# Token mixing of a two-layer hybrid backbone: whole-head score banks, bursts of small products, and work moved between engines

## The chip, the core and the metric

One core of one Trainium2 chip runs the whole program in one launch. The time is device microseconds (us) of that core, the median over runs. The engines are named as in the profile: PE is the matrix engine and PEld its weight loads, DVE the vector engine, ACT the scalar engine, POOL is GpSimd, SP issues most transfers.

## What is computed

Two layers of a hybrid backbone run over 1024 latent tokens and 256 context tokens of width 1024. Each layer mixes tokens and then applies a gated convolutional feed-forward network. The change is in the mixing, whose parts are these (from the reference, cut):

```python
def attend(q, k, v):
    s = jnp.einsum('bhgqd,bhkd->bhgqk', q, k).astype(jnp.float32) * (HEAD_DIM ** -0.5)
    p = jax.nn.softmax(s, axis=-1).astype(v.dtype)
    return jnp.einsum('bhgqk,bhkd->bhgqd', p, v)
...
def gla_scan(q, k, v, logf, s0, reverse):
    ...
    def step(state, inp):
        ...
        scores = jnp.einsum('bhtk,bhtsk,bhsk->bhts', qc, decay, kc)
        o = (jnp.einsum('bhts,bhsv->bhtv', scores, vc)
             + jnp.einsum('bhtk,bhkv->bhtv', qc * jnp.exp(cum), state))
```

There are eight attention heads of width 64. A latent token reads 1280 keys, a context token 256. The recurrence has four heads and runs forward and backward, with a decay for every channel. A Fourier mix over the tokens is the third part. The three results are joined and pass through one output projection.

## The kernel before

**Stages.** In each layer the kernel projects the queries, keys and forget gates (`project_qkv`), and then starts the attention as a generator that is laced with whatever else the mixing has to do: the remaining projections (`project_rest`), the Fourier mix (`fourier`), the recurrence (`recurrence`) and the first output tiles. `interleave` advances the attention in proportion to shares in the table `LACE`. The feed-forward network follows. In the profiled execution the attention of the first layer lies between about 286 and 757 us and its recurrence between 520 and 750 us; in the second layer the attention lies between 2037 and 2467 us and the recurrence between 2280 and 2465 us.

**What sets the order.** Each engine takes its instructions strictly in a fixed order. A scheduler makes that order ahead of time from the order of the code, the dependencies, and a priority: `ahead("qk")` and the like move the instructions of a `with` block forward by the number in the table `AHEAD`. An instruction that stands early and is not ready holds up everything behind it on its engine.

**Attention.** `score(i, pr)` handles two heads of one 128-row tile. For one head it takes the 1280 keys in pieces of 512, 512 and 256. Each piece has a PSUM bank of its own (tag `s`, three banks, used in turn), two products on PE into it (L567 and L568), and a maximum over the piece on DVE (L570). A fourth small maximum joins the three (L573). Then ACT takes the exponential of each piece (L577), which also reads out a sum. `value(i, pr)` transposes the exponentials on PE (`ps_t`, L603), splits them into a rounded part `ph` (ACT, L608) and a rest `pl` (DVE, L609), and multiplies both with the values (`ps_o`, L613 and L615).

**Recurrence.** `pair_steps(i)` handles two tiles of 128 tokens, and at most two pairs are in work at once. A pair goes through seven levels. A level forms small products of the decayed queries and keys (`scores`, tile `psc`, L774): 64 channels deep, 32 or 64 tokens wide, 16 or 32 of them for a level, alternately for the two halves `e` of the channels, each half in a PSUM bank of its own (tag `g`, two banks, which the other small results of the mixing use too). In the profile each of these products is two matrix instructions. The results go into `near` (L857), `next` (L861) or `at` (L864). Then four products with the decays update the tile `W` for the next level (L876): the one with `w == 0` on DVE, the other three on POOL. At the level of 32 tokens eight copies on DVE put `near` and `next` into `at` (L868). `kc` is copied from `W` on ACT (L838) for the next level's products.

## Time and profile before

| what | value |
|---|---|
| median of 3 runs | 3351.05 us (3343.71 to 3359.85) |
| the profiled execution, its own time | 3347.55 us |
| its span in the trace | 3345.0 us |
| PE busy, share of the span | 3087.2 us, 92% |
| DVE busy | 2379.1 us, 71% |
| ACT busy | 1581.3 us, 47% |
| POOL busy | 780.8 us, 23% |
| granted clock of PE, mean | 0.973 |

The shares are means over stages that differ. PE counts as busy as long as any matrix instruction is in flight, from the start of the first to the modelled end of the last. A time between two starts on PE therefore tells more of what an instruction costs than its own length does, since the instructions overlap.

### The profile page before, as it was taken

What the parts mean: (1) busy time and instruction counts of PE and PEld (TensorE: products, weight loads), DVE (VectorE), ACT (ScalarE), POOL (GpSimd) and SP (SyncE); (2) the same over time, 40 slices, a digit from 0 to 9 for tenths busy, and PEclk for the clock granted to TensorE, in tenths of its full rate; (3) what the DMA queues carried; (4) which work ended last, traced back from release to release, by engine and by line L of the source; (5) the groups of instructions that cost most, each with busy time, mean ns of one, the idle gap of its engine ahead of it and who ended that gap; (6) DMA issues with size and microseconds to landing.
All of it is one profiled execution on the core that took longest, in us unless ns stands there. A gap on an engine that the chain in (4) does not pass through costs nothing.

```text
span 3345.0 us, 55178 instructions
## 1 busy us (share of the span) xinstructions
PE 3087.2 (92%) x20897; PEld 2517.1 (75%) x20897; DVE 2379.1 (71%) x4377; ACT 1581.3 (47%) x3169; POOL 780.8 (23%) x820
## 2 busy tenths in 40 slices
PE   6999998999979999899999999998988789999996
PEld 4878977787756777677798788876766577887785
DVE  4624567887688877567876754668877778887678
ACT  3324556674444444334464435655652435554332
POOL 3522114432210000021245351115435200000222
PEclk9999998999989999999999999999999899999998
DMA  7652232107665444597775432122035632223973
GB/s 216 193 164 81 61 98 58 39 16 227 210 196 164 128 131 128 167 244 196 232 215 177 133 101 76 46 86 76 20 98 168 208 111 85 86 76 116 276 187 126
DMA packets 449215, 452.83 MB, mean 135 GB/s; under 512 B 31731, under 2 KB 343476, under 8 KB 448950
## 3 DMA queue, kind: packets, MB, share of 16 engines
q1 hardware_dynamic: 420118, 405.05, 38.6%
q0 software_dynamic: 28832, 44.27, 7.1%
q8 instruction: 164, 2.69, 0.3%
q14 instruction: 101, 0.83, 0.1%
HBM read 354.68 MB, written 94.54 MB: 134 GB/s over the span
## 4 chain that ended last, share of the span: by engine, by line
PE 46%; DVE 12%; DMA 5%; POOL 3%; issue 2%; ACT 2%; SPq 0%; POOLq 0%; DVEq 0%; ACTq 0%
PE pu L159 8%; PE pu L160 8%; PE pu L161 8%; PE pd L159 3%; PE pd L160 3%; PE pd L161 3%; PE ps_t L603 2%; DMA araw<-act 2%; DVE cv L1106 1%; PE ps_s L567 1%; PE ps_o L613 1%; PE ps_s L568 1%; PE ps_o L615 1%; PE pws L159 1%; DVE wlo L1373 1%
## 5 line engine op out<-in xcount | busy, mean ns | idle before, releaser
L570 DVE TENSOR_REDUCE mx<-ps_s 128x1 f32<-128x512 f32 (+1 forms) x400 | 222.0, 587 | 104.6 <-PE ps_s L568 103.3
L1331 POOL DMA_DIRECT2D X<-in_w_down_dram x48 | 57.0, 1188 | 1022.5 <-DMA X<-in_w_down_dram 944.7
L609 DVE TENSOR_TENSOR pl<-ps_t,ph 128x512 fp32r<-128x512 f32 x328 | 222.8, 685 | 84.1 <-ACT ph L608 82.2
L603 PE MATMUL ps_t<-ident,p 128*128 128x128 f32 x1312 | 260.2, 282 | 13.7 <-DVE pl L609 8.1
L577 ACT ACTIVATE p<-ps_s,mx 128x512 f32<-128x512 f32 (+1 forms) x400 | 242.4, 615 | 52.7 <-DVE mx L573 43.2
L608 ACT CAST ph<-ps_t 128x512 fp32r<-128x512 f32 x328 | 190.5, 588 | 158.8 <-PE ps_o L615 81.8
L160 PE MATMUL pd<-wlo,whi 128*128 128x512 f32 x616 | 248.6, 404 | 14.6 <-DVE wlo L1373 12.9
L159 PE MATMUL pd<-whi,wlo 128*128 128x512 f32 x616 | 243.6, 402 | 17.5 <-DVE wlo L1373 10.4
L1106 DVE SCALAR_TENSOR_TENSOR cv<-U,cw,cv 128x512 f32<-128x512 f32 x352 | 246.7, 746 | 12.8 <-ACT cv L1103 12.7
L161 PE MATMUL pd<-whi 128*128 128x512 f32 x616 | 248.1, 403 | 0.0
L159 PE MATMUL pxs<-whi,hlo 128*128 128x256 f32 x752 | 220.9, 294 | 5.7 <-DVE hraw L1552 4.3
L145 POOL TENSOR_TENSOR wlo<-raw,whi 128x1024 fp32r<-128x1024 f32 x63 | 153.5, 2439 | 281.1 <-ACT whi L144 281.0
L160 PE MATMUL pxs<-wlo,hhi 128*128 128x256 f32 x752 | 215.9, 287 | 0.5 <-DVE wlo L145 0.4
L161 PE MATMUL pxs<-whi,hhi 128*128 128x256 f32 x752 | 215.8, 287 | 0.0
L613 PE MATMUL ps_o<-pl,V 128*128 128x256 f32 x656 | 199.5, 321 | 7.0 <-DVE pl L609 4.1
L603 PEld LDWEIGHTS ps_t<-ident,p 128*128 128x128 f32 x1312 | 163.8, 142 | 36.8 <-DVE pl L609 11.1
L1103 ACT ACTIVATE cv<-U,cb,cw 128x512 f32<-128x512 f32 x176 | 137.6, 812 | 111.8 <-DVE U L1234 99.4
L615 PE MATMUL ps_o<-ph,V 128*128 128x256 f32 x656 | 182.0, 295 | 0.0
L1218 ACT CAST whi<-S 128x512 fp32r<-128x512 f32 x176 | 106.1, 618 | 146.4 <-PE pu L161 110.4
L144 ACT CAST whi<-raw 128x1024 fp32r<-128x1024 f32 x130 | 135.8, 1047 | 81.9 <-DMA raw<-in_w_up_dram 30.1
L567 PE MATMUL ps_s<-KT,qt 128*128 128x512 f32 (+1 forms) x400 | 149.8, 405 | 6.5 <-ACT p L577 3.1
L159 PEld LDWEIGHTS pd<-whi,wlo 128*128 128x128 f32 x616 | 117.6, 192 | 49.7 <-DVE wlo L1373 13.1
(398 smaller groups left out, 9191.7 us busy)
## 6 DMA issues: line engine op xcount, KB each, us to landing
raw<-in_w_up_dram SPq DMA_DIRECT2D x144, 512.0 KB
raw<-in_w_ada_dram SPq DMA_DIRECT2D x96, 512.0 KB
raw<-in_w_down_dram SPq DMA_DIRECT2D x52, 512.0 KB
act<-cv SPq DMA_DIRECT2D x88, 256.0 KB
X<-in_w_down_dram POOLq DMA_DIRECT2D x40, 512.0 KB, 9.7
raw<-in_w_in_dram SPq DMA_DIRECT2D x36, 512.0 KB
y<-r SPq DMA_DIRECT2D x28, 512.0 KB
araw<-act SPq DMA_DIRECT2D x26, 512.0 KB
```

What stands on the lines that cost most here:

```text
L159: nc.tensor.matmul(o, lhsT=al, rhs=bh, start=start, stop=False, skip_group_check=onto)
L160: nc.tensor.matmul(o, lhsT=ah, rhs=bl, start=False, stop=False, skip_group_check=onto)
L161: nc.tensor.matmul(o, lhsT=ah, rhs=bh, start=False, stop=stop, skip_group_check=onto)
L567: nc.tensor.matmul(t[:, 0:n], lhsT=qt[:, h % (2 * QT_PAIRS), :], rhs=KT[:, 2 * kv + 1, s0:s0 + n], start=True, stop=False)
L570: nc.vector.tensor_reduce(out=mx[:, j:j + 1], in_=t[:, 0:n], axis=AX.X, op=ALU.max)
L577: nc.scalar.activation(out=t, in_=sc[j][:, 0:n], func=AF.Exp, bias=mx[:, 3:4], accum_out=su[:, h, j:j + 1])
L603: nc.tensor.transpose(t[:, ss, h, :], in_=ps2[h][2 * s2 + ss], identity=ident)
L608: nc.scalar.copy(ph, tv)
L609: nc.vector.tensor_tensor(out=pl, in0=tv, in1=f32(ph), op=ALU.subtract)
L613: nc.tensor.matmul(o, lhsT=V[:, s, kv, 1:3, :].rearrange("p a c -> p (a c)"), rhs=pl[:, ss, :], start=(s == 0), stop=False)
L615: nc.tensor.matmul(o, lhsT=V[:, s, kv, 0:2, :].rearrange("p a c -> p (a c)"), rhs=ph[:, ss, :], start=False, stop=(s == nk - 1))
L1106: nc.vector.scalar_tensor_tensor(out=o, in0=u[:, tap:tap + n], scalar=convw[l][tap][:, c:c + 1], in1=o, op0=ALU.mult, op1=ALU.add)
```

## The change

- `score`: one tile of three banks holds all scores of a head; there is one such tile (`bufs=1`). The products stand as before, two for each bank. One maximum over all 1280 scores and one exponential over them follow, with one sum. The exponentials of a head lie in one buffer, five of these in all (before ten of 512 and five of 256, the same bytes).
- `AHEAD`: the score products, the maximum, the exponential and the small products of the recurrence all get 200 in both layers.
- `scores`: the half `e = 1` now comes first, and all other products of a call are ordered behind that first one (`tc.issue_after`).
- `pair_steps`: all four products with the decays go to POOL where outputs are needed (the one with `w == 2` stays on DVE for context tiles of the last layer), and the eight copies into `at` go to ACT.

```diff
--- before.py
+++ after.py
@@ -49,8 +49,8 @@
     {"p1": 0.578, "ft": 0.08, "hg": 0.38, "p3": 6.415, "pair": 3.177, "lead": 8.4},
 )
 AHEAD = (
-    {"qk": 50, "max": 100, "exp": 0, "pt": 50, "split": 0, "pv": 0, "kc": 0, "psc": 0, "ev": 50, "w": 0},
-    {"qk": 150, "max": 50, "exp": 0, "pt": 30, "split": 0, "pv": 0, "kc": 10, "psc": 0, "ev": 0, "w": 30},
+    {"qk": 200, "max": 200, "exp": 200, "pt": 50, "split": 0, "pv": 0, "kc": 0, "psc": 200, "ev": 50, "w": 0},
+    {"qk": 200, "max": 200, "exp": 200, "pt": 30, "split": 0, "pv": 0, "kc": 10, "psc": 200, "ev": 0, "w": 30},
 )
 R_AT = (4, 6)
 DOWN_AT = ((("P34", "P35", "P23", "P24"), ("P21", "P22", "P24", "P25"), ("P21", "P22", "P24", "P25"), ("P21", "P22", "P23", "P24")),
@@ -60,7 +60,7 @@
 QT_PAIRS = 1
 QT_BUFS = 3
 IN_WP = 2
-P_BUFS = {512: 10, 256: 5}
+P_BUFS = 5
 
 C_Q, C_KV, C_HQ, C_HI, C_FF, C_FB, C_HG, C_FT = 0, 512, 768, 1024, 1280, 1536, 1792, 2048
 
@@ -545,10 +545,9 @@
 
         def score(i, pr):
             nk = keys(i)
-            segs = [(s, min(512, nk * P - s)) for s in range(0, nk * P, 512)]
-            ns = len(segs)
+            n = nk * P
             if pr == 0:
-                su = ap.tile([P, NH, 3], F32, tag="su", bufs=2, name="su")
+                su = ap.tile([P, NH], F32, tag="su", bufs=2, name="su")
                 state["su", i] = su
             su = state["su", i]
             if pr % QT_PAIRS == 0:
@@ -559,31 +558,26 @@
             kv = pr // 2
             ps2 = []
             for h in (2 * pr, 2 * pr + 1):
-                mx = ap.tile([P, 4], F32, tag="mx", bufs=4, name="mx")
-                sc, p = [], []
-                for j, (s0, n) in enumerate(segs):
-                    t = psn.tile([P, 512], F32, tag="s", bufs=3, name="ps_s")
+
+                mx = ap.tile([P, 1], F32, tag="mx", bufs=4, name="mx")
+                t = psn.tile([P, 3 * 512], F32, tag="s", bufs=1, name="ps_s")
+                for s0 in range(0, n, 512):
+                    sl = slice(s0, min(n, s0 + 512))
                     with ahead("qk" if (i, pr) != units[0] else "pt"):
-                        nc.tensor.matmul(t[:, 0:n], lhsT=qt[:, h % (2 * QT_PAIRS), :], rhs=KT[:, 2 * kv + 1, s0:s0 + n], start=True, stop=False)
-                        nc.tensor.matmul(t[:, 0:n], lhsT=qt[:, h % (2 * QT_PAIRS), :], rhs=KT[:, 2 * kv, s0:s0 + n], start=False, stop=True)
-                    with ahead("max"):
-                        nc.vector.tensor_reduce(out=mx[:, j:j + 1], in_=t[:, 0:n], axis=AX.X, op=ALU.max)
-                    sc.append(t)
+                        nc.tensor.matmul(t[:, sl], lhsT=qt[:, h % (2 * QT_PAIRS), :], rhs=KT[:, 2 * kv + 1, sl], start=True, stop=False)
+                        nc.tensor.matmul(t[:, sl], lhsT=qt[:, h % (2 * QT_PAIRS), :], rhs=KT[:, 2 * kv, sl], start=False, stop=True)
                 with ahead("max"):
-                    nc.vector.tensor_reduce(out=mx[:, 3:4], in_=mx[:, 0:ns], axis=AX.X, op=ALU.max, negate=True)
-                for j, (s0, n) in enumerate(segs):
-                    t = ap.tile([P, n], F32, tag=f"p{n}", bufs=P_BUFS[n], name="p")
-                    with ahead("exp"):
-                        nc.scalar.activation(out=t, in_=sc[j][:, 0:n], func=AF.Exp, bias=mx[:, 3:4],
-                                             accum_out=su[:, h, j:j + 1])
-                    p += [t[:, c:c + P] for c in range(0, n, P)]
+                    nc.vector.tensor_reduce(out=mx, in_=t[:, 0:n], axis=AX.X, op=ALU.max, negate=True)
+                e = ap.tile([P, NT * P], F32, tag="p", bufs=P_BUFS, name="p")
+                with ahead("exp"):
+                    nc.scalar.activation(out=e[:, 0:n], in_=t[:, 0:n], func=AF.Exp, bias=mx, accum_out=su[:, h:h + 1])
+                p = [e[:, c:c + P] for c in range(0, n, P)]
                 ps2.append(p)
                 yield 0.84e-3 * nk * P
             state["p", i, pr] = ps2
             if pr == NH // 2 - 1:
                 rs = ap.tile([P, NH], F32, tag="rs", bufs=2, name="rs")
-                nc.vector.tensor_reduce(out=rs, in_=su[:, :, 0:ns], axis=AX.X, op=ALU.add)
-                nc.vector.reciprocal(out=rs, in_=rs)
+                nc.vector.reciprocal(out=rs, in_=su)
                 t = psn.tile([P, 512], F32, tag="g", bufs=2, name="ps_rs")
                 nc.tensor.transpose(t[0:NH, 0:P], in_=rs, identity=ident)
                 rt = ap.tile([NH, P], F32, tag="rst", bufs=2, name="rst")
@@ -767,12 +761,15 @@
 
 
             ts = [pg([P, 2, 2, size], "psc") for _ in range(2)]
-            for x in range(2):
-                for c in range(2):
-                    for b in range(0, P, size):
-                        for e in range(2):
-                            nc.tensor.matmul(ts[e][b:b + size, x, c, :], lhsT=keys(slice(64 * e, 64 * e + 64), c, x * P + b),
-                                             rhs=moving(slice(64 * e, 64 * e + 64), c, x * P + b), start=True, stop=True)
+            after = nullcontext()
+            for x, c, b, e in product(range(2), range(2), range(0, P, size), (1, 0)):
+
+                with after:
+                    m = nc.tensor.matmul(ts[e][b:b + size, x, c, :], lhsT=keys(slice(64 * e, 64 * e + 64), c, x * P + b),
+                                         rhs=moving(slice(64 * e, 64 * e + 64), c, x * P + b), start=True, stop=True)
+                if x == c == b == 0 and e:
+                    first = m.ins
+                after = tc.issue_after(first)
             return ts
 
         def advance(st, first, tot, u, i):
@@ -865,12 +862,12 @@
                     if h == 32:
                         for b in range(0, P, 32):
                             for src, o in ((near, b), (next_, b ^ 32)):
-                                nc.vector.tensor_copy(at[b:b + 32, :, :, :, o:o + 32], src[b:b + 32])
+                                nc.scalar.copy(at[b:b + 32, :, :, :, o:o + 32], src[b:b + 32])
                     yield 0.6
                 for (w, side, d) in ((0, 1, 0), (1, 0, 1), (3, 1, 1), (2, 0, 0)):
                     if w < 2 and not need_o:
                         continue
-                    eng = nc.vector if w == 0 or not need_o and w == 2 else nc.gpsimd
+                    eng = nc.vector if not need_o and w == 2 else nc.gpsimd
                     w5 = W5[:, w, :, :, side, :]
                     with ahead("w"):
                         eng.tensor_tensor(out=w5, in0=w5, in1=tv[:, d, :, :, 1 - side, None].to_broadcast([P, 2, nb, h]), op=ALU.mult)
```

The order of PE's instructions near the end of the first layer's recurrence, before (`psc` are the small products, `ps_t` transposes, `ps_s` the scores of a head, `ps_o` the products with the values):

```order
L774 MATMUL psc<-W 64x64 x8
L603 MATMUL ps_t<-ident,p 128x128
L774 MATMUL psc<-W 64x64 x2
L603 MATMUL ps_t<-ident,p 128x128
L774 MATMUL psc<-W 64x64
L603 MATMUL ps_t<-ident,p 128x128
L774 MATMUL psc<-W 64x64
L603 MATMUL ps_t<-ident,p 128x128
L774 MATMUL psc<-W 64x64 x4
L567 MATMUL ps_s<-KT,qt 128x512
L568 MATMUL ps_s<-KT,qt 128x512
```

The same place on PE after the change:

```order
L567 MATMUL ps_s<-KT,qt 128x512
L768 MATMUL psc<-W 32x32 x32
L568 MATMUL ps_s<-KT,qt 128x512
L567 MATMUL ps_s<-KT,qt 128x512
L568 MATMUL ps_s<-KT,qt 128x512
L567 MATMUL ps_s<-KT,qt 128x256
L568 MATMUL ps_s<-KT,qt 128x256
L597 MATMUL ps_t<-ident,p 128x128
L768 MATMUL psc<-W 64x64 x16
L597 MATMUL ps_t<-ident,p 128x128 x3
L607 MATMUL ps_o<-pl,V 128x256
```

The last level's 16 products stood in five pieces and now stand in one. Over the whole program the small products stand in 220 pieces before and in 130 after; pieces of one or two products are 97 of the 220 and 18 of the 130.

The order of PE where the first layer's recurrence begins, after the change, from the end of one head's scores to the beginning of the next head's:

```order
L568 MATMUL ps_s<-KT,qt 128x256
L597 MATMUL ps_t<-ident,p 128x128 x5
L607 MATMUL ps_o<-pl,V 128x256
L609 MATMUL ps_o<-ph,V 128x256
L607 MATMUL ps_o<-pl,V 128x256
L609 MATMUL ps_o<-ph,V 128x256
L768 MATMUL psc<-q,kc 32x32 x17
L567 MATMUL ps_s<-KT,qt 128x512
L568 MATMUL ps_s<-KT,qt 128x512
L567 MATMUL ps_s<-KT,qt 128x512
```

Between the heads stand five transposes, four products with the values and 17 small products. Before the change the products of a head's banks stand apart, each behind the exponential of its own bank.

The third place is PE inside the recurrence of the first layer, before, where the numbers tell the two banks of one level's products apart (8154 and 8155):

```order
L615 MATMUL ps_o_8140<-ph_8146,V_385 128x256
L774 MATMUL psc_8154<-q_8049,kc_8063 32x32 x16
L603 MATMUL ps_t_8271<-ident_64,p_7901 128x128
L603 MATMUL ps_t_8271<-ident_64,p_8044 128x128
L603 MATMUL ps_t_8271<-ident_64,p_7901 128x128
L603 MATMUL ps_t_8271<-ident_64,p_8044 128x128
L774 MATMUL psc_8155<-q_8049,kc_8063 32x32 x16
```

And such a place after the change:

```order
L768 MATMUL psc_8624<-W_8349,kc_8620 32x32 x16
L607 MATMUL ps_o_8275<-pl_8421,V_385 128x256
L597 MATMUL ps_t_8533<-ident_64,p_8134 128x128
L768 MATMUL psc_8623<-W_8349,kc_8620 32x32 x16
L609 MATMUL ps_o_8275<-ph_8420,V_385 128x256
```

Here the 32 products of one level stand as two halves of 16, one for each bank and so one for each half of the channels, with other work between them. Such pieces of 16 products of one bank number 7 before and 53 after.

## Rows read from the trace of the kernel before

**Rows 1.** Page, part 1, whole program: busy us, share, instructions of each engine

```profile
PE 3087.2 (92%) x20897; PEld 2517.1 (75%) x20897; DVE 2379.1 (71%) x4377; ACT 1581.3 (47%) x3169; POOL 780.8 (23%) x820
```

**Rows 2.** Stretches of the mixing: length, then busy us and instructions by engine, clock

```profile
520.00:740.00 220.00, 201.66 (x3403) 164.09 (x3400) 182.14 (x451) 148.05 (x409) 101.40 (x135) 0.95 0.15 39
2030.00:2230.00 200.00, 198.30 (x1382) 174.82 (x1380) 125.62 (x262) 127.69 (x327) 28.01 (x28) 1.00 0.23 68
2280.00:2460.00 180.00, 165.85 (x2751) 134.01 (x2750) 152.65 (x363) 118.60 (x321) 80.63 (x104) 0.99 0.10 26
```

**Rows 3.** Who PE waited for, 520 to 740: us in total, times, longest

```profile
PE psc L774 <- DVE mx L573: 3.7, 6, 1.2
...
PE psc L774 <- POOL W L876: 1.0, 1, 1.0
...
PE ps_o L613 <- DVE ob L621: 0.3, 1, 0.3
```

**Rows 4.** The same view, 2280 to 2460

```profile
PE psc L774 <- DVE near L857: 1.7, 1, 1.7
...
PE ps_t L603 <- DVE pl L609: 0.3, 1, 0.3
```

**Rows 5.** Timeline of PE near 736 us: start, length, instruction, count

```profile
730.25 0.60 PE L603 MATMUL ps_t<-ident,p 128*128 128x128 f32 x4
...
735.71 0.33 PE L603 MATMUL ps_t<-ident,p 128*128 128x128 f32 x1
735.97 0.33 PE L774 MATMUL psc<-W 64*64 64x64 f32 x4
...
736.49 0.32 PE L774 MATMUL psc<-W 64*64 64x64 f32 x2
...
737.26 0.33 PE L603 MATMUL ps_t<-ident,p 128*128 128x128 f32 x1
```

**Rows 6.** Timeline of PE near 648 us

```profile
647.25 0.28 PE L613 MATMUL ps_o<-pl,V 128*128 128x256 f32 x1
647.37 0.28 PE L615 MATMUL ps_o<-ph,V 128*128 128x256 f32 x1
647.58 0.45 PE L774 MATMUL psc<-q,kc 64*32 64x32 f32 x32
647.97 0.66 PE L603 MATMUL ps_t<-ident,p 128*128 128x128 f32 x4
```

**Rows 7.** Weight loads of tile psc, whole program: ns min/median/max

```profile
L774 PEld LDWEIGHTS psc<-W,kc x2880: 102/106/155, 529.1 to 2438.9; 64*32 64x32 f32 x192
```

**Rows 8.** Groups by line and shape, 520 to 740: count, busy us, mean ns, idle before

```profile
L570 DVE TENSOR_REDUCE mx<-ps_s 128x1 f32<-128x512 f32 x63 | 41.8, 683 | 10.0 <-PE ps_s L568 9.8
L570 DVE TENSOR_REDUCE mx<-ps_s 128x1 f32<-128x256 f32 x31 | 12.8, 413 | 2.2 <-PE ps_s L568 2.2
L573 DVE TENSOR_REDUCE mx<-mx 128x1 f32<-128x3 f32 x31 | 4.5, 144 | 0.1
L577 ACT ACTIVATE p<-ps_s,mx 128x512 f32<-128x512 f32 x64 | 43.8, 689 | 5.5 <-DVE mx L573 5.1
L577 ACT ACTIVATE p<-ps_s,mx 128x256 f32<-128x256 f32 x31 | 14.9, 480 | 0.2
L577 ACT ACTIVATION_READ_ACCUMULATOR p<-ps_s,mx 128x1 f32 x94 | 19.1, 204 | 0.0
L876 POOL TENSOR_TENSOR W<-W,tot 128x256 f32<-128x256 f32 x90 | 59.2, 676 | 94.5 <-PE psc L774 59.4 <-DVE tot L878 15.5 <-ACT kc L838 12.3
L876 DVE TENSOR_TENSOR W<-W,tot 128x256 f32<-128x256 f32 x30 | 19.1, 636 | 0.2
L868 DVE COPY at<-near 32x256 f32<-32x256 f32 x20 | 7.2, 359 | 0.2
L864 ACT COPY at<-psc 64x256 f32<-64x256 f32 x20 | 6.3, 367 | 1.2 <-PE psc L774 1.1
```

**Rows 9.** Who waited for tile ps_s, whole program: us in total, times

```profile
  PEld ps_s L567: 21.7, 78
```

## The prediction

> **What bounds the kernel now.** Start with the page: PE is busy for 92% of the span and no other engine comes near [rows 1]. That is a mean over stages, so the second look is at the stretches of the mixing, the only place where the order of instructions changes. While the projections run beside the attention (2030 to 2230), PE is busy for 198.30 of 200 us: nothing but less work on PE helps there. In the recurrence PE is idle for 18.3 us of 220 in the first layer and for 14.2 us of 180 in the second, and DVE is busy for 83% and 85% of them [rows 2]. The third look is at whom PE waits for there. In the first layer ten rows name DVE, 11.1 us together, and in the second eight rows, 8.6 us; the first and the last of each stand in [rows 3, 4]. The small products wait for POOL's decay products once, for 1.0 us [rows 3]. The fourth look is at the starts of PE's instructions one by one, since an engine that is busy may still lose time at each change of work [rows 5, 6]. So the mixing is bound by PE's queue: by its work, by the cost of switching to small products and back, and by short waits for a crowded DVE.
>
> **The change, part by part.** The sum is made against the profiled execution, 3347.55 us.
>
> *Bursts of small products.* Four transposes in a row start 0.11 us apart (0.60 us less the last one's 0.27, over three) [rows 5]. With small products between them, three transposes and three pieces of 4, 2 and 2 products (the middle rows of one repeated pattern are left out) take 737.26 - 735.71 = 1.55 us. Less 0.33 for the transposes and some 0.07 for eight products, that is 0.38 us a piece. A long piece costs less: a product with the values starts 0.12 us behind its neighbour, but 0.21 us pass before the small products behind it start, and 0.39 us from there to the next transpose [rows 6], of which 32 products at 0.009 take 0.29. That makes 0.09 + 0.10, about 0.2 us. The order has 90 pieces less (220 to 130), and 79 of these are of one or two products, so they are nearer to the dear kind, although the dear rows are the widest products. I take 0.28: **-25 us**, with ends at -18 and -34. All of this is PE's own time, so nothing hides it.
>
> A half burst of one bank (third place of the order) might be slow, and it isn't: that piece of 32 matrix instructions, all of one half of the channels, took 0.45 us [rows 6]. The Trainium skill ("TensorE: Matmul & The Clock Gate", Part 3, "The mechanism") says that a weight load overlaps matrix products in flight only where it uses other rows of the array. By that rule the 53 half bursts would each wait for 32 loads in turn, and the sum would come out on the other side; the time is with the rivals. The trace disagrees here, 0.45 us against the 3.4 us of 32 loads.
>
> *DVE in the recurrence.* A head's maxima cost 2 x 683 + 413 + 144 = 1.92 us on DVE [rows 8]. One maximum over 1280 follows from the slope between 256 and 512, (683 - 413)/256 = 1.05 ns for each element: 683 + 768 x 1.05 = 1.49 us. In the first layer's recurrence DVE loses 31 x 0.43 = 13 us by that, 21 us by the products with `w == 0` (30 x 0.64 and five of another shape), and 14 us by the copies (40, of which the half shown has a mean of 0.36). DVE falls from 182 us to some 134, or 61% of the stretch. Of PE's 19.7 us of waits for DVE I take two thirds: **-13 us**, ends 0 and -20. What is late next is the exponential on ACT.
>
> *One exponential and the copies on ACT.* A head costs ACT 2 x 689 + 480 + 3 x 204 = 2.47 us [rows 8], of which the reads of the sums overlap a little. One exponential over 1280 takes, by the slope, 689 + 768 x 0.82 = 1.32 us, and one read 0.2. The eight copies of a pair move to ACT at 0.36 to 0.37 us each (the DVE copy and the nearest ACT copy, 64 rows high [rows 8]): 40 x 0.37 = 15 us more in the first layer's recurrence, against some 30 us less. ACT at 148 of 220 us covers them: **0 us**. If that cover is gone, it is because `ph` stands behind an exponential that is twice as long; this belongs to the next part.
>
> *Scores in three banks with one buffer.* The next head's first score product now waits for the whole exponential of this head, where it waited for that of one bank. From the last score product: 0.28 us for itself (a product as wide as those of [rows 6]), 1.49 for the maximum, 1.32 for the exponential and 0.1 of the read that follows it: **3.2 us a head**. Before, it was 0.28 + 0.41 + 0.14 + 0.69 + 0.1, some 1.6 us, and even so PE's weight loads waited for an exponential 78 times, for 21.7 us [rows 9], mostly while other products were still in flight. I summed PE's work between one head's scores and the next head's along the new order, with 0.11 us for a transpose, 0.12 for a product with the values and so on. In the second place shown that is 5 x 0.11 + 4 x 0.12 + about 0.5, some 1.5 us. Of 127 such intervals 66 hold less than 3.2 us, and 38 us are missing in all. Only 7 of the 38 lie in the stretches where projections keep PE full; the others lie where PE stands idle now and then for other operands in any case. Against that, the second and third bank no longer wait for anything. I take **+10 us**, ends 0 and +38.
>
> *The fourth product on POOL.* 63 products move (7 levels of 9 pairs), at 0.68 us against 0.64 on DVE [rows 8]. A level on POOL now takes four in turn, 2.7 us, where it took three beside the one on DVE. POOL rises from 101 to some 125 us of 220. It was idle for 59.4 us there because it waited for the small products, not the other way round [rows 8]. I take **+3 us**; below, nothing speaks for a gain; above, each level may be late by a whole product, 63 x 0.68 = +43.
>
> *Sum:* -25 - 13 + 10 + 3 = -25 us, or 3322.5 against 3347.55. The median of the runs before stands 3.5 us above the profiled execution, so the **median forecast is 3326 us**. What a measurement of this kernel can tell from no change is about 0.5%, 16.8 us.
>
> **The rivals.**
> 1. *The long chain of a head stops PE (slower).* The place is PE's queue at the first score product of each head. For it: 66 intervals are shorter than the chain even if neither DVE nor ACT has anything else to do, and a maximum that stands behind a 0.68 us instruction on DVE, or an exponential behind a cast on ACT, comes later still. Against it: both engines get emptier. The other terms without my +10 are -35 us, so it decides from 35/128 = 0.27 us a head, and makes the kernel measurably slower from 0.41. At 0.6 us a head it is 77 - 35 = +42: **3393 us**.
> 2. *POOL becomes what a level waits for (no change).* The next level's products need all four results, and they now stand early in PE's queue. At 0.4 us for each of 63 levels, 25 us take back the whole gain: **3351 us**. For it: four products in turn. Against it: POOL's idle time, above.
> 3. *PE's idle time in the recurrences nearly goes (larger gain).* 32.5 us of idle time and the dear price of the pieces, 34: **3285 us**. Against it: some of that idle time is the start of the recurrence, where nothing is ready.
> 4. *Half bursts run load by load.* 53 x (3.4 - 0.45) = 156 us on PE, with 32 loads at 0.106 us [rows 7]: 3351 - 25 + 156, about **3480 us**. The row of 0.45 us speaks against it [rows 6]. The rule of the Trainium skill cited above would make it so.
>
> **How the numbers follow.** The forecast gets 0.47, with a range of its own from 3308 to 3334. Rival 3 gets 0.12, rival 2 gets 0.26, rival 1 gets 0.13 and rival 4 gets 0.02. Faster by over 0.5% (below 3334) is 0.47 + 0.12 = 0.59; within it 0.26; slower 0.13 + 0.02 = 0.15. The range takes in the forecast, most of rival 3 and of rival 2, and leaves out rivals 1 and 4 and the outer ends: 3286 to 3362.
>
> **What would show it.** Right: far fewer pieces of `psc` between transposes in the timeline; DVE near 60% in the recurrences; DVE's rows among PE's waits shrunk; `mx` at about 1.5 us and `p` at about 1.3. Wrong: `ps_s L567 <- ACT p` among the longest waits of PE, above all between 2030 and 2230, where PE is idle for 1.7 us in all; or `psc <- POOL W` there with tens of us; or the stretches as long as before with PE busier.

## The result, and the profile after

The changed kernel takes 3375.08 us (median of 5 runs, 3370.73 to 3385.12) against 3353.27 us of the kernel before on the same chip: a ratio of 1.0072, 95% interval 1.0057 to 1.0087. It is slower by 0.72%, where 3326 us was forecast. The profiled execution's span is 3373.3 us, 28.3 more than before. The first and last starts of the tiles on PE tell where they went (us, before and after):

| stretch on PE | first layer | second layer |
|---|---|---|
| first score product to last projection product | 163.7, 175.6 | 177.3, 176.8 |
| from there to the first small product (Fourier mix) | 76.9, 83.3 | 76.3, 86.4 |
| from there to the first product of the output projection | 234.8, 236.0 | 189.1, 187.9 |

The recurrences, where the forecast expected nearly all of its 25 us, are as long as before, though they hold 13 and 12 score products fewer, some 2 to 3 us of PE each, which now stand in the stretches before them. The loss lies in the first layer's projections and in both Fourier stretches. The page's first part, and the stretches that answer to [rows 1, 2]:

```profile
PE 3091.9 (92%) x20897; PEld 2532.8 (75%) x20897; DVE 2293.6 (68%) x3824; ACT 1545.5 (46%) x2729; POOL 815.8 (24%) x883
```

```profile
520.00:740.00 220.00, 188.13 (x3216) 158.57 (x3218) 143.84 (x269) 139.30 (x307) 116.11 (x163) 0.93 0.15 41
2030.00:2230.00 200.00, 198.93 (x1357) 178.40 (x1356) 101.78 (x129) 103.96 (x178) 27.54 (x27) 1.00 0.20 59
2280.00:2460.00 180.00, 152.54 (x2576) 125.86 (x2575) 124.33 (x230) 107.26 (x233) 97.14 (x137) 0.90 0.16 45
```

DVE fell to 65% of the first stretch, near the 61% that was forecast. PE, however, is idle for 31.9 and 27.5 us where it was for 18.3 and 14.2, and its granted clock fell from 0.99 to 0.90 in the second layer. (The recurrences begin 17 and 29 us later than before, so these windows hold less of them. From each kernel's own first small product to its first product of the output projection, PE is idle for 32.4 and 27.1 us, before for 21.1 and 21.3, at a granted clock of 0.93 and 0.91, before 0.96 and 0.97.) Whom PE waits for, 520 to 740 and then 2280 to 2460 (total, times, longest; answers to [rows 3, 4]):

```profile
PE psc L768 <- POOL W L873: 5.8, 6, 2.8
PE psc L768 <- POOL kc L816: 5.4, 1, 5.4
PE ps_s L567 <- ACT p L573: 5.1, 6, 1.5
PE psc L768 <- DVE near L854: 4.3, 5, 1.9
...
PE ps_t L597 <- DVE pl L603: 3.0, 5, 0.8
```

```profile
PE ps_t L597 <- DVE pl L603: 6.2, 6, 3.4
PE psc L768 <- DVE near L854: 6.0, 6, 1.9
PE psc L768 <- POOL W L873: 5.8, 9, 1.7
```

`mx` is gone from these lists. In its place stand links by which one level of the recurrence hands over to the next (`W` on POOL, `near`) and the exponential `p`. `W` and `p` are the two kinds of row that the prediction named as signs of its failure, though `W` with less than tens of us in a stretch, and `p` not between 2030 and 2230, where PE is still idle for only 1.1 us. The wait for `kc` is no such link: it is one wait before the very first small products, which now stand early in PE's queue and are not ready. The timeline of PE has it:

```profile
543.97 0.55 PE L768 MATMUL psc<-q,kc 64*32 64x32 f32 x34 [5.37 <-POOL kc L816]
```

PE stands idle for 5.4 us there, and for 3.4 us at the same place of the second layer, where the view names no releaser; before it was 0.9 us and none. So some 8 of the 16.5 us by which the two Fourier stretches grew are idle time in front of the first burst. The costs of single instructions, by shape, 520 to 740 (answers to [rows 8]):

```profile
L873 POOL TENSOR_TENSOR W<-W,tot 128x256 f32<-128x256 f32 x108 | 68.3, 656 | 53.8 <-PE psc L768 30.9 <-DVE tot L875 11.2 <-ACT kc L835 10.5
L570 DVE TENSOR_REDUCE mx<-ps_s 128x1 f32<-128x1280 f32 x31 | 46.0, 1485 | 8.5 <-PE ps_s L568 8.4
L573 ACT ACTIVATE p<-ps_s,mx 128x1280 f32<-128x1280 f32 x31 | 41.2, 1330 | 9.0 <-PE ps_t L597 5.7 <-DVE mx L570 3.2
...
L865 ACT COPY at<-near 32x256 f32<-32x256 f32 x16 | 6.4, 402 | 0.9 <-DVE near L854 0.7
```

The maximum (1.49 us forecast), the exponential (1.32) and the copies (0.37) came out nearly as priced. What was wrong is what these instructions do to waits.

**PE's time in three parts.** From the first score product to the first output product of both layers, each time between two starts on PE was compared with the usual one (the 40th percentile) of the same two kinds of instruction at full clock, over all the traces of this study. What is over that, in a stretch of low clock, up to the usual time at low clock, is put down to the clock; the rest is waits. The columns are us; "pieces" counts the runs of small products in the planned order. Differences between rows mean something, the level of the last column (which holds ordinary scatter) does not. They are good to some 5 us: drawing the kinds a little differently moves single entries by up to 10 us and the differences used below by at most 5.

| kernel | pieces | work and switches | low clock | waits |
|---|---|---|---|---|
| before | 220 | 746 | 11 | 161 |
| changed | 130 | 727 | 24 | 195 |
| changed, without the bursts | 236 | 756 | 36 | 189 |
| before with the bursts | 117 | 719 | 14 | 187 |
| before with the W product on GpSimd | 256 | 757 | 21 | 168 |
| before with the three-bank scores | 234 | 754 | 19 | 181 |
| before without maxima | 273 | 758 | 20 | 150 |
| the same with priority 200 | 148 | 725 | 18 | 170 |
| copies on ACT, two W products on GpSimd | 197 | 740 | 12 | 170 |
| the same with the bursts | 127 | 722 | 15 | 174 |

### The profile page after: what moved, and what is told of

The parts are those of the page before. It is cut to its first block, busy times and chain, and to the rows that moved or that the text cites. A ratio compares the mean times of both kernels' runs of the same rounds, so it can differ in the third digit from the quotient of the medians.

```text
span 3373.3 us, 54332 instructions
## 1 busy us (share of the span) xinstructions
PE 3091.9 (92%) x20897; PEld 2532.8 (75%) x20897; DVE 2293.6 (68%) x3824; ACT 1545.5 (46%) x2729; POOL 815.8 (24%) x883
## 5 line engine op out<-in xcount | busy, mean ns | idle before, releaser
L570 DVE TENSOR_REDUCE mx<-ps_s 128x1 f32<-128x1280 f32 (+1 forms) x144 | 197.1, 1369 | 111.7 <-PE ps_s L568 111.1
L160 PE MATMUL pd<-wlo,whi 128*128 128x512 f32 x616 | 248.6, 404 | 14.2 <-DVE wlo L1370 14.0
L597 PE MATMUL ps_t<-ident,p 128*128 128x128 f32 x1312 | 243.3, 284 | 12.2 <-DVE pl L603 11.2
L573 ACT ACTIVATE p<-ps_s,mx 128x1280 f32<-128x1280 f32 (+1 forms) x144 | 177.9, 1236 | 67.5 <-PE ps_t L597 36.6
L567 PE MATMUL ps_s<-KT,qt 128*128 128x512 f32 (+1 forms) x400 | 160.8, 402 | 13.5 <-ACT p L573 10.2
L873 POOL TENSOR_TENSOR W<-W,tot 128x256 f32<-128x256 f32 x222 | 139.7, 655 | 128.8 <-PE psc L768 67.1
```

The lines of the kernel that those rows point to most:

```text
L160: nc.tensor.matmul(o, lhsT=ah, rhs=bl, start=False, stop=False, skip_group_check=onto)
L567: nc.tensor.matmul(t[:, sl], lhsT=qt[:, h % (2 * QT_PAIRS), :], rhs=KT[:, 2 * kv + 1, sl], start=True, stop=False)
L570: nc.vector.tensor_reduce(out=mx, in_=t[:, 0:n], axis=AX.X, op=ALU.max, negate=True)
L573: nc.scalar.activation(out=e[:, 0:n], in_=t[:, 0:n], func=AF.Exp, bias=mx, accum_out=su[:, h:h + 1])
L597: nc.tensor.transpose(t[:, ss, h, :], in_=ps2[h][2 * s2 + ss], identity=ident)
```

## Experiments 1 to 4: each part undone in the changed kernel

Without the three-bank scores:

```diff
-                t = psn.tile([P, 3 * 512], F32, tag="s", bufs=1, name="ps_s")
+                    t = psn.tile([P, 512], F32, tag="s", bufs=3, name="ps_s")
...
-    {"qk": 200, "max": 200, "exp": 200,
+    {"qk": 50, "max": 100, "exp": 0,
```

> The changed kernel, but with the scores of a head in three single banks, three maxima and three exponentials as before (and the old priorities of the score products, the maximum and the exponential). Theory 'scores' (the chain of one buffer for a head stops PE, and costs more than the whole loss): some 3345 us or less. Theory 'POOL' (what PE loses is the wait of small products for decay products on GpSimd): within 6 us of the changed kernel, 3369 to 3381. Theory 'bursts' (an early burst that isn't ready holds PE up): within 8 us of 3375. By the prediction's terms (three banks +10, relief of DVE part of -13) it would be about the same as the changed kernel.

Without the bursts:

```diff
-            for x, c, b, e in product(range(2), range(2), range(0, P, size), (1, 0)):
-                with after:
...
+                        for e in range(2):
...
-"psc": 200
+"psc": 0
```

> The changed kernel, but with the small products in the old order, not held together and without the priority of 200. Theory 'bursts' (an early burst that isn't ready holds PE up, more than the saved pieces give back): 3355 or less. Theories 'scores' and 'POOL' (the bursts' own saving of about 25 us is there, and something else outweighs it): some 3390 to 3400, that is slower than the changed kernel.

With `w == 0` on DVE:

```diff
-                    eng = nc.vector if not need_o and w == 2 else nc.gpsimd
+                    eng = nc.vector if w == 0 or not need_o and w == 2 else nc.gpsimd
```

> The changed kernel, but the decay product with w == 0 is on DVE again. Theory 'POOL': 3350 to 3360, since PE's waits for POOL's W products (7.3 and 6.8 us in the two recurrences) and for what lies behind them go. Theories 'scores' and 'bursts': 3370 to 3380, no difference that can be measured. By the prediction's terms (+3 for POOL, DVE's relief of 21 us): 3375 or a few us more.

With the copies into `at` on DVE:

```diff
-                                nc.scalar.copy(at[b:b + 32, :, :, :, o:o + 32], src[b:b + 32])
+                                nc.vector.tensor_copy(at[b:b + 32, :, :, :, o:o + 32], src[b:b + 32])
```

> The changed kernel, but the eight copies of a pair into at are on DVE again. All theories: within 5 us of the changed kernel, 3370 to 3380; if DVE's relief by them is worth what the prediction says of DVE, 3 us more.

Measured, as ratios to before (the change: 1.0072): without the three banks 1.0066 (1.0049 to 1.0083), without the bursts 1.0168 (1.0153 to 1.0183), with W on DVE 1.0057 (1.0042 to 1.0072), with the copies on DVE 1.0124 (1.0109 to 1.0139). In this company the bursts are worth 32 us and the copies on ACT 17 (where all theories had expected less than 5), as differences of ratios times 3350; both are true gains. No theory of a single cause holds: taking away the three banks or the W product alone changes the time by less than the intervals tell. Taking away the three banks moves the loss, though. By the same starts as in the table above, the stretches before the recurrences are then as long as before the change (163.9 and 177.4, 76.5 and 76.6 us), and the first layer's recurrence takes 257.7 us, the second's 186.8. So in the changed kernel the three banks lengthen the stretches before by 28 us and shorten the first recurrence by 22 (12 score products less are some 2 of these). Why they shorten it was not tested.

## Experiments 5 to 8: parts alone on the kernel before

The bursts alone:

```diff
+            for x, c, b, e in product(range(2), range(2), range(0, P, size), (1, 0)):
...
+                after = tc.issue_after(first)
...
-"psc": 0
+"psc": 200
```

> The kernel before, with the bursts alone (the small products of a call behind their first, e = 1 first, priority 200). Theory 'prediction' (each edit adds its term): -25 us, about 3326. Theory 'cover' (the bursts cure what the other edits bring, and give nothing by themselves): within 8 us of before. Theory 'early burst' (it stands before its operands are ready and holds up the transposes behind it; the copies on ACT and the long chain hide that in the changed kernel): slower than before, 3365 or more.

The same, and the copies on ACT:

```diff
-                                nc.vector.tensor_copy(at[b:b + 32, :, :, :, o:o + 32], src[b:b + 32])
+                                nc.scalar.copy(at[b:b + 32, :, :, :, o:o + 32], src[b:b + 32])
```

> The kernel before, with the bursts and the copies on ACT, but scores in single banks and the decay product with w == 0 on DVE as before. Theory 'either of two' (the three-bank scores and the W product on GpSimd each cost the loss, and taking only one away leaves the other in its place): about 25 + 17 us less than before, 3305 to 3325. Theory 'early burst': some 3360 to 3370, as long as without the three-bank scores alone.

The three-bank scores with their priorities alone:

```diff
-                    t = psn.tile([P, 512], F32, tag="s", bufs=3, name="ps_s")
+                t = psn.tile([P, 3 * 512], F32, tag="s", bufs=1, name="ps_s")
...
-    {"qk": 50, "max": 100, "exp": 0,
+    {"qk": 200, "max": 200, "exp": 200,
```

> The kernel before, with only the scores of a head in three banks (one maximum, one exponential, their priorities of 200). Theory 'prediction': some +10 for the chain less 13 x 13/48 = 4 for DVE's relief, +6 us, 3356. Theory 'shared stall' (the long chain stops PE only where the bursts and POOL do not already): +30 us or more, 3380. Theory 'early burst': within 10 us of before.

The product with `w == 0` on GpSimd alone:

```diff
-                    eng = nc.vector if w == 0 or not need_o and w == 2 else nc.gpsimd
+                    eng = nc.vector if not need_o and w == 2 else nc.gpsimd
```

> The kernel before, with only the decay product with w == 0 moved to GpSimd. Theory 'prediction': +3 us less 6 for DVE's relief, no difference that can be measured. Theory 'either of two' or 'shared stall': +15 to +30 us, 3365 to 3380. Theory 'early burst': within 8 us of before, as the products stand late in PE's queue there.

Measured: bursts alone 0.9996 (0.9984 to 1.0008); bursts and copies 0.9997 (0.9984 to 1.0009); three banks alone 1.0072 (1.0057 to 1.0087), +24 us; W alone 1.0077 (1.0060 to 1.0094), +26 us. So **either of the two edits costs by itself as much as the whole change loses**, and the bursts, by themselves, give nothing. By the same starts as in the first table, the W product loses 12 and 14 us in the two recurrences and nothing elsewhere; the three banks lose 12 us in the first layer's projections, 3 and 6 in the Fourier stretches and 7 in each recurrence (35 in sum, of which the profiled execution has 7 back elsewhere). Neither theory on bursts with copies had their time, 3353 us.

Singly (three banks, W, and bursts with copies) the parts come to +49, together to +24. Two kernels of experiments 1 to 4 tell more, since each is the bursts and copies with one of the two costs:

| on the kernel before | without bursts and copies | with both |
|---|---|---|
| nothing else | 1 | 0.9997 |
| three banks | 1.0072 | 1.0057 |
| W product on GpSimd | 1.0077 | 1.0066 |
| three banks and W | not run | 1.0072 |

Beside one of the two costs the bursts and copies give back 4 or 5 us, no more than the intervals tell. The second cost, where the first is there with bursts and copies, adds 2 to 5 us: the two overlap.

## Experiments 9 to 11: the bursts' priority, the chain of a head

```diff
-"psc": 0
+"psc": 200
```

> The kernel before, with only the priority of the small products raised to 200 (no ordering behind the first, e = 0 first as before). In the planned order the small products stand in 122 pieces on PE, with the bursts as changed 117, before 220. Theory 'density' (PE saves the switches between kinds of products and waits for DVE, ACT and POOL instead): within 8 us of before, as the bursts as changed, PE's switches less by some 27 us and waits more by as much. Theory 'e first' (the order of the two halves makes the wait): 8 to 25 us faster than before.

```diff
-    {"qk": 200, "max": 200, "exp": 200,
+    {"qk": 50, "max": 100, "exp": 0,
```

> The kernel before, with the scores of a head in three banks, but with the old priorities of the score products, the maximum and the exponential. Theory 'chain' (the next head's first score product waits for the chain of one buffer, however the queue is sorted): +20 to +35 us on before, and the first layer's stretch with projections some 10 us longer, as with the priorities of 200. Theory 'priority' (the score products stand too early in PE's queue): less than +10 us, and that stretch as long as before.

```diff
-                with ahead("max"):
-                    nc.vector.tensor_reduce(out=mx, in_=t[:, 0:n], axis=AX.X, op=ALU.max, negate=True)
...
-                    nc.scalar.activation(out=e[:, 0:n], in_=t[:, 0:n], func=AF.Exp, bias=mx, accum_out=su[:, h:h + 1])
+                    nc.scalar.activation(out=e[:, 0:n], in_=t[:, 0:n], func=AF.Exp, scale=1e-3, accum_out=su[:, h:h + 1])
```

> The kernel before with the scores in three banks and their priorities of 200, but the maximum over a head's scores is left out (the exponential takes a scale of 0.001 instead, to keep numbers finite), so the chain from the last score product to the free buffer is about 1.4 us shorter, and DVE has some 1.4 us less for each head. Theory 'chain': the first layer's stretch with projections is as long as before (163 to 165 us from the first score product to the last projection product, where the kernel with the three banks takes 175.7), and the whole at least 20 us faster than with the maximum, 3350 or less. Theory 'priority': that stretch stays above 170 us.

The priority alone: 0.9987 (0.9974 to 1.0000), with 122 pieces; the ordering behind the first product and the order of the halves add nothing that these runs show. Three banks with the old priorities: 1.0056 (1.0037 to 1.0076), so the three banks themselves and not the priorities are most of their cost. Without the maximum: 1.0012 (0.9999 to 1.0026), 20 us less. Against the kernel before without maxima (0.9989, below) the three banks then cost 8 us, where they cost 24 with them. Leaving out the maximum shortens the chain and also relieves DVE, and the two are not told apart here. The result agrees with the theory of the chain for the whole, but not for its place: the first layer's stretch with projections stayed long there (174.9 us from the first score to the last projection product, 170.0 with the old priorities, 175.7 with both). The timeline of the changed kernel shows the chain, PE, DVE and ACT for one head in that stretch (start, length, instruction, idle time before it and what ended it):

```profile
364.42 0.29 PE L568 MATMUL ps_s<-KT,qt 128*128 128x256 f32 x1
...
364.74 1.49 DVE L570 TENSOR_REDUCE mx<-ps_s 128x1 f32<-128x1280 f32 x1 [3.32 <-PE ps_s L568]
...
366.27 1.33 ACT L573 ACTIVATE p<-ps_s,mx 128x1280 f32<-128x1280 f32 x1
...
367.50 0.19 ACT L573 ACTIVATION_READ_ACCUMULATOR p<-ps_s,mx 128x1 f32 x1
...
367.74 0.19 PEld L567 LDWEIGHTS ps_s<-KT,qt 128*128 128x128 f32 x1 [0.16 <-ACT p L573]
```

From the last score product to the next head's first are 3.32 us (forecast 3.2). With the priority of 200 that first product stands on PE before the exponential has ended for nearly every head: in the stretch of the kernel with the three banks alone its weights are loaded 0.05 us behind the end of the exponential's readout in 36 of 39 cases. These 39 products start 12.3 us in all behind their neighbours, where 0.12 us each would be 4.7, so some 8 of the 12 us are short waits at a head's beginning, mostly while the products before it are in flight, where the list of waits does not show it. Without the maximum a head's first product stands earlier still, 1.70 us (median) behind the last score product instead of 3.32, and it starts 0.05 us behind the readout in 37 of 39 cases: the shorter chain is met by an earlier product. In the second layer's stretch with projections it is 29 of 32 cases, but there 20 of 30 heads waited so before the change (in the first layer 2 of 24), and nothing is lost.

## Experiments 12, 15 and 18: how many products in turn on GpSimd

All three on the kernel with the bursts and the copies on ACT, which has three of the four products of a level on GpSimd. One carries out `w == 1` twice, the others leave two or one on GpSimd:

```diff
-                        eng.tensor_tensor(out=w5, in0=w5, in1=tv[:, d, :, :, 1 - side, None].to_broadcast([P, 2, nb, h]), op=ALU.mult)
+                        for _ in range(2 if w == 1 else 1):
+                            eng.tensor_tensor(out=w5, in0=w5, in1=tv[:, d, :, :, 1 - side, None].to_broadcast([P, 2, nb, h]), op=ALU.mult)
```

```diff
-                    eng = nc.vector if w == 0 or not need_o and w == 2 else nc.gpsimd
+                    eng = nc.vector if w < 2 or not need_o and w == 2 else nc.gpsimd
```

```diff
-                    eng = nc.vector if w == 0 or not need_o and w == 2 else nc.gpsimd
+                    eng = nc.vector if (w != 2 if need_o else w == 2) else nc.gpsimd
```

> The kernel with the bursts and the copies on ACT (about the time of before), with one of the three decay products on GpSimd, w == 1, carried out twice; so GpSimd has four products in turn at each level as in the change, and DVE keeps the one with w == 0. The second pass multiplies by the decay once more, which changes the result, not the work. Theory 'four in turn' (a level waits for GpSimd's fourth product): 15 to 25 us slower than without the second pass, 3368 to 3378, as with w == 0 moved (3369.6 in that company). Theory 'order' (the move of w == 0 costs by the other order that it makes on DVE and PE, not by GpSimd's time): within 6 us of 3353.

> The kernel with the bursts and the copies on ACT, and with the decay products w == 0 and w == 1 on DVE, so that GpSimd has two in turn at a level, where it has three there and four in the change. Theory 'recurrence chain' (a level waits for the last product on GpSimd): 10 to 25 us faster than with three, 3328 to 3343, as the fourth cost 28. Theory 'DVE sets the waits': slower by 5 to 20 us, 3358 to 3375, since DVE gets 20 us more in each recurrence.

> The bursts and the copies on ACT, with three decay products on DVE and one on GpSimd. Theory 'balance' (DVE now has three in turn, 1.9 us at a level, and its 20 us more in each recurrence stand before the maxima and the rests that PE waits for): 3345 to 3365, slower than with two and two. Theory 'GpSimd only' (each product off GpSimd is worth 15 us or more): 3320 or less.

Measured: with four in turn 1.0087 (1.0067 to 1.0106), three 0.9997, **two 0.9944 (0.9925 to 0.9964)**, one 0.9976 (0.9965 to 0.9988). The view of the tile `psc` says how long PE and its weight loads, added up, stood idle before the small products until a decay product of POOL ended (us, times): before, then four, three, two and one in turn.

```profile
  POOL W L876: 10.8, 19
```

```profile
  POOL W L880: 45.1, 46
```

```profile
  POOL W L879: 25.0, 29
```

```profile
  POOL W L879: 4.6, 10
```

```profile
  POOL W L879: 2.6, 6
```

In the changed kernel, with four in turn, it is 41.8 us, 52 times. Four in turn cost 30 us more than three here with almost the same number of pieces (140 and 136) and all of DVE's products in place, so it is the longer turn on GpSimd that costs. With one on GpSimd this wait is nearly gone, and the kernel is still 10 us slower than with two; that the three on DVE cost them fits the theory of the balance, and no run shows it apart. Two and two, at 3336.44 us, is faster than both kernels of this case.

## Experiments 13, 14, 16 and 17: why the bursts alone give nothing

Without maxima, with the small products' priority at 0 and at 200; the priority of 200 in the second layer only; and the two-and-two split without the bursts (the edit of experiment 15 and the copies on ACT, on the kernel before):

```diff
-                        nc.vector.tensor_reduce(out=mx[:, j:j + 1], in_=t[:, 0:n], axis=AX.X, op=ALU.max)
...
-                        nc.scalar.activation(out=t, in_=sc[j][:, 0:n], func=AF.Exp, bias=mx[:, 3:4],
+                        nc.scalar.activation(out=t, in_=sc[j][:, 0:n], func=AF.Exp, scale=1e-3,
```

```diff
-    {"qk": 150, "max": 50, "exp": 0, "pt": 30, "split": 0, "pv": 0, "kc": 10, "psc": 0, "ev": 0, "w": 30},
+    {"qk": 150, "max": 50, "exp": 0, "pt": 30, "split": 0, "pv": 0, "kc": 10, "psc": 200, "ev": 0, "w": 30},
```

> The kernel before with all maxima over the scores left out (the exponentials take a scale of 0.001 instead); banks, bursts and priorities as before. DVE has 1.9 us a head less in one go, and the exponential no longer waits for it. Theory 'DVE sets the waits' (the prediction's second term): 13 to 25 us faster than before, 3328 to 3340. Theory 'recurrence chain' (PE waits for the chain of levels over GpSimd, and any other wait is in its shadow): within 6 us of before. In the planned order the small products stand in 273 pieces here, 53 more, which costs 15 us of PE by the price of a piece; so a time as before would leave it open, unless the waits of PE fall by as much.

> The same without maxima, with the priority of 200 for the small products: 148 pieces for 273. Theory 'DVE sets the waits': the saved switches count now, 125 pieces x 0.28 = 35 us less than without the priority, and at least 20 us less than before. Theory 'recurrence chain': within 10 us of the kernel without maxima and without the priority; PE's waits for POOL W grow instead.

> The kernel before, with the priority of 200 for the small products in the second layer only. In the profile of the kernel with 200 in both layers the first layer lost 6 us from its first score to its output products and the second gained 6. Both theories: 5 to 8 us faster than before, 3344 to 3347, if these differences are the plan's and not of one execution; within 3 us of before if not.

> The kernel before with the copies on ACT and two decay products on DVE and two on GpSimd (its time with the bursts is 3336), without the bursts; 197 pieces of small products in the plan for 127. Theory 'recurrence chain' (with three on GpSimd the bursts gave nothing because the levels' chain was the bound; with two, PE is the bound again): 12 to 25 us slower than with the bursts, 3348 to 3361. Theory 'all from GpSimd' (the shorter turn is worth 16 us whatever PE's order): 3331 to 3341.

Measured: no maxima 0.9989 (0.9975 to 1.0004); with the priority 0.9941 (0.9921 to 0.9962); two and two without the bursts 0.9990 (0.9979 to 1.0001); the priority in the second layer only 0.9967 (0.9956 to 0.9979), 11 us, a version that is faster than both kernels too. Set side by side, the bursts (or their priority) are worth: 1 to 4 us on the kernel before, 16 where DVE has no maxima, 15 where GpSimd has two products in turn, 32 in the company of the change's other parts. PE's saving in work and switches is 18 to 33 us each time (table above). What differs more is the waits. On the kernel before they grow by 26 us, with two in turn on GpSimd by 4: there the theory of the recurrence's chain holds. Without maxima they still grow by 20, and the gain comes from a larger saving, 33 us for 125 pieces less; so the theory of DVE holds in part at most. Why the waits hardly grow in the change's own company was not separated.

The sum also hides the layers. With the bursts alone the first layer's mixing, from its first score product to its first product of the output projection, takes 483.6 us, before 475.5, and the second layer's 435.7, before 442.8. So in the second layer the saving does count, and the priority there alone is worth 11 us; in the first layer the bursts lose 8. Why the layers differ was not tested.

## Why the prediction was wrong, point by point

- **Bursts, -25 us: the size of the saving was right, the sum was not.** PE's work and switches fall by 27 us with the bursts alone. (The pieces of 4, 2 and 2 in the forecast's working are matrix instructions, so 2, 1 and 1 products; the price of a piece stands.) The step that failed is "All of this is PE's own time, so nothing hides it". By the table of PE's time the waits grow by 26 us as the switches go, above all in the first layer, which gets longer, while the second gets shorter. The likely reading is that the loose pieces stood where PE would have waited in any case, and that bursts leave these waits bare.
- **DVE's relief, -13 us: not there.** DVE became nearly as empty as forecast. The step that failed is "Of PE's 19.7 us of waits for DVE I take two thirds": only the waits for `mx` went, and those for `near` and `pl`, which hang on the level's chain and on ACT, grew. Counted over each kernel's own recurrences, PE waits 23.1 us for DVE, before 17.8, and 27.3 for POOL, before 10.4. Taking away all maxima on the kernel before gave 0.9989: the waits fall by 11 us, about the size forecast, and the planned order, now with 273 pieces, takes 12 us back in switches and 9 in clock. (That makes the mixing 10 us longer in this execution, and the rest of it is 11 us shorter, which stays unexplained.) With the small products' priority at 200, which keeps the pieces together, the same edit is worth 15 us (0.9987 to 0.9941). So the price left out is that of a new plan. The edit takes more off DVE than the change does, so it does not price the change's own relief.
- **One exponential, and copies on ACT, 0: the prices of the instructions were right, the company was not.** The copies are worth nothing beside the bursts alone and 17 us in the changed kernel.
- **Three banks, +10 us: 24.** The chain was forecast at 3.2 us and is 3.3. "Only 7 of the 38 lie in the stretches where projections keep PE full" is the step that failed: 12 us were lost in the first layer's such stretch alone, some 8 by a short wait for nearly every head and some 2 by 12 more score products that fall into it. Rival 1 had this mechanism, and priced it at 77 us. Whether the one buffer or the joined maximum and exponential make most of the chain's cost, no run separates.
- **The fourth product on POOL, +3 us: 26.** Rival 2 named it with 25 us. The argument against it, the step that failed, ("idle ... because it waited for the small products, not the other way round") read POOL's idle time as slack. With bursts and copies it is not: the two wait for each other in one chain, and a product more in turn costs 30 us, one less gains 18, as the waits for `W` go from 25.0 us to 45.1 or 4.6. For the move on the kernel before, rival 2's number is partly luck: of the 28 us in the table only 7 are waits, 11 are work and switches (256 pieces for 220) and 10 low clock.
- **The clock, not in the sum: +13 us.** Large products run slower where the granted clock is low. More waits don't explain it by themselves: with the bursts alone the waits grow by 26 us and the low clock costs 3, with W alone they grow by 7 and it costs 10. What brings the clock down stays open.
- **The half bursts** (rival 4) cost nothing to speak of: with 53 of them, PE's work and switches are 29 us less than without the bursts.

The likeliest case was therefore a sum of terms of which two were taken for independent gains and two for small costs. The runs show two costs of 24 and 26 us which overlap: with bursts and copies they are 20 and 23 singly and 25 together. The bursts alone give nothing in sum, and are worth 32 us in the company of both costs and the copies. How they overlap is known by place (with bursts and copies the loss of the three banks lies before the recurrences, that of the W product in the first of them), not by cause.

## What to carry to other kernels

An engine that is 92% busy can still be one link of a chain; saving its work pays only as far as the chain behind it gets shorter too, so price the next waiter before counting a saving. Where a planner fixes the order, every edit makes a new plan: compare the counts of pieces and the waits of both plans, and test parts alone and undone, since their worth depends on company. Each time here is that of one plan; no run shows how far two plans of the same edit would differ. When a job can go to either of two engines, count how many stand in turn on each: here two and two beat three and one, and four in turn were worst.

## What the runs showed of the hardware

**The clock.** Two stretches of the changed kernel, 14 us apart, with their granted clock (the column before the last two), and PE's products at the low one:

```profile
2349.20:2362.80 13.60, 11.96 (x251) 9.61 (x243) 6.76 (x14) 9.19 (x22) 11.07 (x19) 0.50 0.08 27
2363.00:2376.00 13.00, 12.69 (x157) 11.62 (x156) 8.99 (x18) 9.33 (x21) 2.72 (x5) 1.00 0.07 17
```

```profile
2349.02 1.08 PE L768 MATMUL psc<-W 64*32 64x32 f32 x64 [1.90 <-DVE near L854]
...
2354.93 1.23 PE L768 MATMUL psc<-W 64*64 64x64 f32 x32 [1.34 <-DVE near L854]
...
2356.67 0.41 PE L607 MATMUL ps_o<-pl,V 128*128 128x256 f32 x1
2356.89 0.41 PE L609 MATMUL ps_o<-ph,V 128*128 128x256 f32 x1
```

0.50 is the level of 1.2 GHz. The products with the values start 0.22 us apart there, 0.12 at full clock [rows 6]. PE had waited 1.90 us just before it and 1.34 us within it. A wait is paid for a second time where the clock falls beside it; that these waits brought it down is not shown.

**One product, two engines.** The prediction took a decay product at 0.64 us on DVE and 0.68 on POOL, from means [rows 8]. The view of tile `W` gives min, median and max (ns), before and after:

```profile
L876 POOL TENSOR_TENSOR W<-W,tot x168: 610/662/1192, 531.2 to 2453.0; 128x256 f32<-128x256 f32 x168
L876 DVE TENSOR_TENSOR W<-W,tot x60: 404/426/1726, 535.8 to 2452.9; 128x256 f32<-128x256 f32 x60
```

```profile
L873 POOL TENSOR_TENSOR W<-W,tot x222: 605/634/923, 550.8 to 2478.4; 128x256 f32<-128x256 f32 x111
```

On DVE it takes 0.43 us as a rule, and now and then up to 1.73. The more of them are on DVE, the longer those on POOL: a mean of 655 ns with nearly none there, 689 before, 738 with two and two, 778 with three on DVE. The Trainium skill ("SBUF — State Buffer", section "Who interferes with whom") says that a DVE instruction with two inputs in SBUF contends with a GpSimd instruction that reads SBUF. The trace agrees, with 655 to 778 ns. No run here separates that contention from other causes.
